# S5 units of a decoder trunk: E turned on TensorE, Toeplitz operand copied out of PSUM, parameter work issued ahead

## The chip, the cores and the metric

One core of a Trainium2 chip runs the whole program. The metric is device time in microseconds: the median of several executions. The profile is that of one further execution.

## The reference

A batch of one, 256 tokens, width 2048, two layers. Layer 0 mixes with an S5 diagonal state space, layer 1 with differential attention on one shared K/V; each layer has a squared-ReLU MLP (2048 to 8192 and back), and sandwich RMS norms stand around every sub-layer. Only the S5 mixer matters here. It has 128 groups of 16 channels with 64 complex states each:

```python
u = (x @ w_in).reshape(Bsz, L, SSM_GROUPS, SSM_GROUP)
# per group: abar = exp(step * lam), bbar = (abar - 1) / lam * b
s_t = abar * s_{t-1} + bbar @ u_t          # complex, 64 states
y_t = Re(c @ s_t) + d_skip * u_t
z = gelu(y)
val, gate = split(z @ w_glu, 2)
mix = val * sigmoid(gate)
```

All matrices are f32, 2048x2048 for w_in and 2048x4096 for w_glu.

## The kernel before

The program is one trace of tile operations. A scheduler at build time orders the instructions of each engine by priority (program order) and by durations that it plans with; at run time every engine's queue is fixed and in order. Work that is ready early can so be placed ahead of work that stands earlier in the program.

In S5, tokens are taken as 32 chunks of 8. Inside a chunk the recurrence is a small matrix (a Toeplitz operand built from a table of the lags 0 to 7); between chunks, states are carried by a scan over 32 chunks.

- Prologue (VectorE): the tables of the groups' parameters: powers of abar (`pw`, written to DRAM as `a_scr` by ScalarE's queue, L447), `Bt`, transposed by TensorE into `T1` and `T2`; chunk rotations `rot`, written to DRAM as `rot_scr`. A zeroed `k_scr` in DRAM is to hold the lag tables; `dskip` holds D on its diagonal.
- `w_in_block(b)`, four of them, each in four steps "W" (L581): u for 512 channels from f32 weights that stream through two buffers (`raw`, on SP's queue, L122), then ScalarE's scaled copy out of PSUM and a VectorE transpose give `Vb`.
- `unit(hh)`, eight of them, 16 groups each, in four steps.
 1. POOL's queue loads `A` (from a_scr) and `B` (from bE); VectorE makes `E` from them (L609 to L612); TensorE multiplies u by E (L615) into `psw`.
 2. POOL loads `cb`; VectorE makes `F` (L627 to L629); TensorE makes the lag table (L634), ScalarE copies it out (`K`, L642), VectorE adds D (L643), and SP's queue writes it to `k_scr` (L645) and reads it back eight times, shifted by a lag each, as the Toeplitz operand `M` (L648).
 3. ScalarE copies psw out (`wsb`, L652), TensorE transposes it into `pst` (L657), and VectorE rotates, scans and rotates back (L667 to L676) and writes the states `ST` (L682, L683). `rt`, the rotations, comes from rot_scr by POOL's queue (L660).
 4. TensorE adds the products with M (L690) and with ST and F (L691) into `psy`, VectorE transposes it (`yT`), ScalarE applies GELU.
- The string `ORDER` gives the program order of W steps and unit steps.
- The GLU follows: `gemm_f32` (L210) takes the first 20 of 32 jobs of its first half in f32 (these need units 0 to 3), all other weights of the trunk are split into a high and a low fp32r part (L137 ScalarE, L138 VectorE) and multiplied at L187 and L188.

The small PSUM tiles of S5 come from one pool of four banks (`mbank`), those of w_in and of the GLU from another of four (`gbank`). The tiles of the units take the memory of the prologue's tiles, and the buffers for split weights take theirs afterwards.

Of the kernel before, what the change touches and what calls it, by code (L numbers as in the profile page):

```python
# [26 lines left out]
ORDER = "WWWW 0000 WWWW 1211122 WW 3 W 2 W 333 WW 4 W 4 W 4455556666 7777"  # L27
P = 128
# [14 lines left out]
def trunk(tc, io, stop=None):  # L43
# [279 lines left out]
    # ------------------------------------------------------------------ S5 layer  # L323
    def s5():
# [14 lines left out]
        dskip = tb.tile([P, 32, SG], F32, name="dskip")  # L339
# [198 lines left out]
        for j in range(4):
            DMA.dma_start(dskip[32 * j : 32 * j + 16], dview(io["d_skip"], j * SG, [[0, 16], [4 * SG, 32], [1, SG]]))
            V.tensor_tensor(  # L540
                dskip[32 * j : 32 * j + 16], dskip[32 * j : 32 * j + 16],
                bc(ident[32 * j : 32 * j + 16, 32 * j : 32 * j + 16], 1, 32), op=MUL,
            )
# [50 lines left out]
        def unit(hh):  # L594
            b, half = divmod(hh, 2)
            par = hh % 2
            g0 = 16 * hh
            Vh = us[b][:, 16 * half : 16 * half + 16, :]
            psw, psk = mbank(), mbank()
            Fs = []  # L600
            for jj in range(2):
# [1 line left out]
                A = ut("A", [8, 2, NS], bufs=2)
                Bq = ut("B", [8, 2, NS], bufs=2)
                a0 = a_scr[0, 0, 0:1]
                nc.gpsimd.dma_start(A.rearrange("p g r n -> p (g r n)"), dview(a0, gj * P, [[G * P, 8], [0, 16], [1, 8 * P]]))
                nc.gpsimd.dma_start(Bq.rearrange("p g r n -> p (g r n)"), dview(io["bE"], gj * P, [[0, 8], [G * P, 16], [1, 8 * P]]))
                E = ut("E", [8, 2, NS])
                V.tensor_tensor(E, bc(A[:, :, 0, :], 2, 2), Bq, op=MUL)  # L609
                V.tensor_tensor(Bq, bc(A[:, :, 1, :], 2, 2), Bq, op=MUL)  # L610
                V.tensor_tensor(E[:, :, 0, :], E[:, :, 0, :], Bq[:, :, 1, :], op=SUB)
                V.tensor_tensor(E[:, :, 1, :], E[:, :, 1, :], Bq[:, :, 0, :], op=ADD)  # L612
# [528 lines left out]
```

## Time and profile before

| | |
|---|---|
| time, median of 3 runs | 2407.84 us (2406.41 to 2408.63) |
| profiled execution, span from first to last instruction | 2406.2 us; its own time is that span and the launch around it, which the record does not give |
| TensorE busy | 2274.4 us (95%) |
| VectorE busy | 1567.2 us (65%) |
| ScalarE busy | 1000.6 us (42%) |
| DMA moved | 432.25 MB, mean 180 GB/s |

Busy shares are means over stages with different limits. The S5 units stand in the first 365 us of the span; everything after them is the GLU's second part, the MLPs, and attention. Read a stage from its own rows: what each engine does there, what it waits for, and what clock TensorE was granted.

### The profile page before, as it was taken

The numbers are of one execution on the slowest core, as the hardware profiler recorded it, in microseconds if no ns is written. First come the engines' busy times: TensorE is split into PE (matmuls) and PEld (weight loads), VectorE is DVE, ScalarE is ACT, GpSimd is POOL, SyncE is SP. The second block draws the span as 40 slices with busy tenths as digits, with TensorE's granted clock in tenths as the row PEclk, the third lists the DMA queues.
The fourth block names the chain that finished last, engine by engine and source line by source line (L and its number), as shares of the span: only waits on it lengthen the run. The fifth ranks groups of instructions, "written<-read, shape, count | busy, mean of one in ns | idle before, by whom it ended". The sixth has DMA issues, their size and how long they took to land.

```text
span 2406.2 us, 32521 instructions
## 1 busy us (share of the span) xinstructions
PE 2274.4 (95%) x13137; PEld 1903.0 (79%) x13137; DVE 1567.2 (65%) x2392; ACT 1000.6 (42%) x1470; POOL 30.4 (1%) x54
## 2 busy tenths in 40 slices
PE   7757689989999999999999999998999999999999
PEld 3335578868888888888868888886888888888887
DVE  8557656867556656656668896656765665665655
ACT  3011125554444444443554455444544444444442
POOL 0100100000000000000000000000000000000000
PEclk9878889999999999999999999999999999999999
DMA  9888976425554554554525544443555555555542
GB/s 282 198 167 159 165 172 248 174 97 210 201 202 173 197 191 174 197 190 158 206 99 188 180 171 162 158 175 123 189 197 210 181 187 192 183 186 192 186 165 104
DMA packets 93943, 432.25 MB, mean 180 GB/s; under 512 B 17377, under 2 KB 39649, under 8 KB 46433
## 3 DMA queue, kind: packets, MB, share of 16 engines
q1 hardware_dynamic: 82624, 405.51, 50.5%
q0 software_dynamic: 9984, 22.04, 4.8%
q10 hardware_dynamic: 1184, 2.62, 0.3%
q8 instruction: 103, 1.69, 0.3%
q14 instruction: 48, 0.39, 0.0%
HBM read 423.44 MB, written 6.68 MB: 179 GB/s over the span
## 4 chain that ended last, share of the span: by engine, by line
PE 85%; DMA 8%; DVE 4%; SPq 1%; ACT 1%; issue 1%; DVEq 0%; ACTq 0%
PE gb L187 47%; PE gb L188 24%; DMA M<-k_scr 4%; DMA raw<-in_w_in_dram 2%; PE gb L184 2%; PE gb L183 2%; PE gb L185 2%; PE mb L256 1%; PE gb L581 1%; DMA k_scr<-K 1%; PE gb L959 1%; PE gb L957 1%; PE gb L958 1%; SPq L648 1%; PE mb L690 1%
## 5 line engine op out<-in xcount | busy, mean ns | idle before, releaser
L138 DVE TENSOR_TENSOR wlo<-raw,whi 128x2048 fp32r<-128x2048 f32 (+1 forms) x540 | 803.1, 1506 | 509.8 <-ACT whi L137 507.6
L137 ACT CAST whi<-raw 128x2048 fp32r<-128x2048 f32 (+1 forms) x540 | 673.3, 1278 | 573.9 <-PE gb L187 375.1
L187 PE MATMUL gb<-x,whi 128*128 128x512 f32 x2400 | 848.8, 398 | 0.0
L188 PE MATMUL gb<-x,wlo 128*128 128x256 f32 x2400 | 675.1, 281 | 0.0
L187 PEld LDWEIGHTS gb<-x,whi 128*128 128x128 f32 x2400 | 450.6, 188 | 109.6
L187 PE MATMUL gb<-xa,whi 128*128 128x512 f32 x1296 | 465.2, 398 | 0.0
L188 PEld LDWEIGHTS gb<-x,wlo 128*128 128x128 f32 x2400 | 453.0, 189 | 0.2
L187 PE MATMUL gb<-xb,whi 128*128 128x512 f32 x1176 | 419.5, 395 | 0.4 <-ACT whi L137 0.4
L188 PE MATMUL gb<-xa,wlo 128*128 128x256 f32 x1296 | 367.8, 284 | 0.0
L188 PE MATMUL gb<-xb,wlo 128*128 128x256 f32 x1176 | 332.0, 283 | 1.6 <-DVE wlo L138 1.6
L187 PEld LDWEIGHTS gb<-xa,whi 128*128 128x128 f32 x1296 | 244.7, 189 | 61.9 <-issue 2.0
L187 PEld LDWEIGHTS gb<-xb,whi 128*128 128x128 f32 x1176 | 221.4, 188 | 52.8 <-issue 2.5
L188 PEld LDWEIGHTS gb<-xa,wlo 128*128 128x128 f32 x1296 | 245.7, 190 | 8.5 <-issue 8.2
L188 PEld LDWEIGHTS gb<-xb,wlo 128*128 128x128 f32 x1176 | 222.9, 190 | 5.2 <-issue 2.9
L215 ACT COPY cr<-gb 128x256 f32<-128x256 f32 x323 | 118.3, 368 | 169.1 <-PE gb L188 167.2
L581 PE MATMUL gb<-raw,h 128*128 128x512 f32 x256 | 122.3, 634 | 23.7 <-DMA raw<-in_w_in_dram 15.6
L162 ACT CAST x<-t 128x256 fp32r<-128x256 f32 x128 | 51.8, 406 | 198.9 <-DVE t L791 174.5
L581 PEld LDWEIGHTS gb<-raw,h 128*128 128x128 f32 x256 | 50.3, 202 | 88.3 <-issue 62.5
L690 PE MATMUL mb<-M,Vb 128*32 128x128 f32 x256 | 36.0, 338 | 76.0 <-DMA M<-k_scr 63.4
L200 DVE TENSOR_TENSOR t<-gb,cr 128x256 f32<-128x256 f32 x151 | 63.1, 418 | 54.9 <-ACT cr L215 54.5
L690 PEld LDWEIGHTS mb<-M,Vb 128*32 128x32 f32 x256 | 19.9, 130 | 82.1 <-issue 78.5
L210 PE MATMUL gb<-z,raw 128*128 128x256 f32 x320 | 72.3, 387 | 2.6 <-DMA raw<-in_w_glu_dram 2.6
(272 smaller groups left out, 2058.5 us busy)
## 6 DMA issues: line engine op xcount, KB each, us to landing
raw<-in_w_up_dram SPq DMA_DIRECT2D x128, 1024.0 KB, 4.7
raw<-in_w_down_dram SPq DMA_DIRECT2D x128, 1024.0 KB, 4.7
raw<-in_w_glu_dram SPq DMA_DIRECT2D x32, 1024.0 KB, 5.1
raw<-in_w_k_dram SPq DMA_DIRECT2D x16, 1024.0 KB, 4.7
raw<-in_w_q_dram SPq DMA_DIRECT2D x16, 1024.0 KB, 4.7
raw<-in_w_v_dram SPq DMA_DIRECT2D x16, 1024.0 KB, 4.7
raw<-in_w_o_dram SPq DMA_DIRECT2D x16, 1024.0 KB, 4.7
raw<-in_w_in_dram SPq DMA_DIRECT2D x15, 1024.0 KB, 10.8
```

What stands on the lines that cost most here:

```text
L137: S.copy(hi[:, c : c + n], raw[:, c : c + n])
L138: V.tensor_tensor(lo[:, c : c + n], raw[:, c : c + n], hi[:, c : c + n].bitcast(F32), op=SUB)
L162: mark[0] = S.copy(dst.hi(dt), src)
L183: T.matmul(ps[:, 0:L], hi[:, c], x.hi(kt), start=f, stop=False)
L184: T.matmul(ps[:, 0:L], hi[:, c], x.lo(kt), start=False, stop=False)
L187: T.matmul(ps, hi[:, c], x.both(kt), start=f, stop=False)
L188: T.matmul(ps[:, L : 2 * L], lo[:, c], x.hi(kt), start=False, stop=l)
L200: V.tensor_tensor(out, ps[:, 0:L], cr, op=ADD)
L210: T.matmul(ps[:, 0:L], w[:, off + kt * P : off + kt * P + P], x[:, kt, :], start=(kt == 0), stop=(kt == nk - 1))
L215: S.copy(cr, ps[:, L : 2 * L])
L581: T.matmul(pss[e], xg[:, kt, e * P : e * P + P], w[:, k4 * 512 : k4 * 512 + 512], start=(kt == 0), stop=(kt == 15))
L690: T.matmul(o, Vh[:, 8 * jj + g, :], M[:, 8 * jj + g, :], start=True, stop=False, tile_position=(0, 32 * g4))
```

## The change

- Parameters: instead of sending the powers of abar through DRAM (`a_scr`, then `A`), TensorE transposes them once, in the prologue, into `AR` and `AI`, which hold them with states on the partitions.
- E: per half unit VectorE forms `X1` (with the states on the partitions) from the b columns of `cb`, which gain a fourth entry (b with its real and imaginary halves swapped), and from AR and AI; TensorE transposes it, eight 128x128 blocks per half unit, and ScalarE copies the result out as `E`. bE is no longer read.
- States: TensorE multiplies E by u directly into `pst` (weights of 64 columns, 32 elements moving), so `psw`, `wsb` and their four transposes go.
- Lag table: 32 columns per matmul instead of 16; the weights are a pair [0, b] or [b, E's lag 1] from `e01`, so that each 32-partition block holds two neighbouring lags. D is added by VectorE in PSUM for both (`dd`). ScalarE then copies the Toeplitz operand `M` straight out of PSUM, 16 copies of 32 partitions, shifted by two lags each; the part of M that is never written was zeroed once by POOL. `k_scr` and `K` go.
- Order: a unit is now `prep` (P, all that needs no u) and `data` (D), and P of a unit stands one or two places ahead of its D. The output matmuls go over four column tiles with M and then four with ST.
- `u` has one buffer instead of two, `Vb` three instead of four.

`rot_scr` and `rt` stay as they are.

```diff
-ORDER = "WWWW 0000 WWWW 1211122 WW 3 W 2 W 333 WW 4 W 4 W 4455556666 7777"
+ORDER = "P0 W W W W P1 W W W W D0 P2 D1 P3 W W W W D2 P4 D3 P5 W W W W D4 P6 D5 P7 D6 D7"
...
         dr = rp("dr", bufs=1, space=DRAM)
-        a_scr = dr.tile([8, G, 2 * NS], F32, name="a_scr")
         rot_scr = dr.tile([P, 2, 64, 32], F32, name="rot_scr")
-        k_scr = dr.tile([G, SG, 15, SG], F32, name="k_scr")
 
...
         rho_n = tb.tile([P, 64], F32, name="rho_n")
-        dskip = tb.tile([P, 32, SG], F32, name="dskip")
...
-        S.dma_start(a_scr.rearrange("d g x -> g d x"), pw[:, 0:8].rearrange("p d r n -> p d (r n)"))
+        nai = ps_.tile([P, 8, NS], F32, name="nai")
+        V.tensor_scalar(nai, pw[:, 0:8, 1, :], -1.0, None, op0=MUL)
+        par = ps_.tile([P, 8, 2, 2, NS], F32, name="par")
+        S.copy(par[:, :, 0, :, :], bc(pw[:, 0:8, 0, :], 2, 2))
+        S.copy(par[:, :, 1, 0, :], nai)
+        S.copy(par[:, :, 1, 1, :], pw[:, 0:8, 1, :])
+        for dst, o in ((AR, 0), (AI, 1)):
+            for d0 in (0, 4):
+                ps = mbank()
+                for i in range(4):
+                    T.transpose(ps[:, i * P : i * P + P], par[:, d0 + i, o].rearrange("p r n -> p (r n)"), ident)
+                S.copy(dst[:, d0 : d0 + 4, :], ps.rearrange("p (d g) -> p d g", g=P))
...
-        zt = ps_.tile([P, SG * 7 * SG], F32, name="zt")
-        V.memset(zt, 0.0)
-        DMA.dma_start(k_scr[:, :, 0:7, :], zt.rearrange("g (p s q) -> g p s q", p=SG, q=SG))
+        pat = ps_.tile([P, 2, SG], F32, name="pat")
+        dskip = ps_.tile([P, 32, SG], F32, name="dskip")
         for j in range(4):
...
+            o = 32 * j
+            S.copy(pat[o : o + 32, 0, :], ident[o : o + 32, o + 16 : o + 32])
+            S.copy(pat[o : o + 32, 1, :], ident[o : o + 32, o : o + 16])
+            DMA.dma_start(dskip[o : o + 32], dview(io["d_skip"], j * SG, [[0, 32], [4 * SG, 32], [1, SG]]))
+        V.tensor_tensor(dd, bc(dskip, 2, 2), bc(pat, 1, 32), op=MUL)
...
+        Mt = [un.tile([P, 16, 8, SG], F32, name=nm("M"), tag=f"M{i}", bufs=1) for i in range(2)]
+        E01 = [un.tile([P, 16, 3, SG], F32, name=nm("E01"), tag=f"E01{i}", bufs=1) for i in range(2)]
+        for i in range(2):
+            GP.memset(Mt[i], 0.0)
+            GP.memset(E01[i][:, :, 0, :], 0.0)
...
-            u = ut("u", [2, 512], bufs=2)
+            u = ut("u", [2, 512], bufs=1)
...
-            Vb = ut("Vb", [32, 32], bufs=4)
+            Vb = ut("Vb", [32, 32], bufs=3)
...
+        def prep(hh):
+            g0 = 16 * hh
             par = hh % 2
-            g0 = 16 * hh
-            Vh = us[b][:, 16 * half : 16 * half + 16, :]
-            psw, psk = mbank(), mbank()
-            Fs = []
+            cb = ut("cb", [16, 4, SG], bufs=2)
+            nc.gpsimd.dma_start(cb, io["cb"][:, g0 * 4 * SG : (g0 + 16) * 4 * SG].rearrange("p (g i q) -> p g i q", i=4, q=SG))
+            e01 = E01[par]
+            psk = mbank()
+            S.copy(e01[:, :, 1, :], cb[:, :, 2, :])
+            Es, Fs = [], []
             for jj in range(2):
                 gj = g0 + 8 * jj
...
-            for jj in range(2):
-                gj = g0 + 8 * jj
-                CR, CI, bS = (cb[:, 8 * jj : 8 * jj + 8, i] for i in range(3))
+                CR, CI, bS, bX = (cb[:, 8 * jj : 8 * jj + 8, i] for i in range(4))
+                X1 = ut("X1", [8, 8, SG], bufs=1)
+                X2 = ut("f2", [8, 8, SG], bufs=2)
+                V.tensor_tensor(X1, bc(bS, 2, 8), bc(AR[:, :, gj : gj + 8].rearrange("p d g -> p g d"), 3, SG), op=MUL)
+                V.tensor_tensor(X2, bc(bX, 2, 8), bc(AI[:, :, gj : gj + 8].rearrange("p d g -> p g d"), 3, SG), op=MUL)
+                V.tensor_tensor(X1, X1, X2, op=ADD)
+                S.copy(e01[:, 8 * jj : 8 * jj + 8, 2, :], X1[:, :, 1, :])
+                E = ut("E", [8, P], bufs=3)
+                for b4 in range(2):
+                    pe = mbank()
+                    for i in range(4):
+                        T.transpose(pe[:, i * P : i * P + P], X1[:, 4 * b4 + i].rearrange("p d q -> p (d q)"), ident)
+                    S.copy(E[:, 4 * b4 : 4 * b4 + 4, :], pe.rearrange("p (g x) -> p g x", x=P))
+                Es.append(E)
                 F = ut("F", [8, 9, SG], bufs=4)
-                f2 = ut("f2", [8, 9, SG], bufs=1)
+                f2 = ut("f2", [8, 9, SG], bufs=2)
                 V.tensor_tensor(F, bc(CR, 2, 9), bc(T1[:, :, gj : gj + 8].rearrange("p d g -> p g d"), 3, SG), op=MUL)
                 V.tensor_tensor(f2, bc(CI, 2, 9), bc(T2[:, :, gj : gj + 8].rearrange("p d g -> p g d"), 3, SG), op=MUL)
                 V.tensor_tensor(F, F, f2, op=ADD)
                 Fs.append(F)
...
+                for sl in (2 * jj, 2 * jj + 1):
+                    for o, n, e0 in ((16, 7, 1), (0, 1, 0)):
+                        for c4 in range(4):
+                            gl = 4 * sl + c4
+                            T.matmul(psk[32 * c4 : 32 * c4 + 32, sl * P + o : sl * P + o + 16 * n],
+                                e01[:, gl, e0 : e0 + 2, :].rearrange("p d q -> p (d q)"),
+                                F[:, gl % 8, 0:n, :].rearrange("p d q -> p (d q)"), start=True, stop=True, tile_position=(0, 32 * c4))
+            kv = psk.rearrange("p (s m q) -> p s m q", s=4, q=SG)
+            V.tensor_tensor(kv[:, :, 0:2, :], kv[:, :, 0:2, :], dd[:, 4 * hh : 4 * hh + 4], op=ADD)
+            M = Mt[par]
+            mv = M.rearrange("p (s c) t q -> p c s t q", c=4)
             for c4 in range(4):
...
+                for j in range(4):
+                    S.copy(mv[32 * j : 32 * j + 32, c4, :, 6 - 2 * j : 8, :], kv[32 * c4 : 32 * c4 + 32, :, 0 : 2 * j + 2, :])
+            held[hh] = Es, Fs, M
+        def data(hh):
+            b, half = divmod(hh, 2)
+            par = hh % 2
+            Es, Fs, M = held.pop(hh)
+            Vh = us[b][:, 16 * half : 16 * half + 16, :]
             pst = mbank()
             for jj in range(2):
-                for ri in range(2):
-                    o = (2 * jj + ri) * P
-                    T.transpose(pst[:, o : o + P], wsb[:, jj, ri].rearrange("p h n -> p (h n)"), ident)
+                for g4 in range(4):
+                    for ri in range(2):
+                        for gh in range(2):
+                            g = 2 * g4 + gh
+                            o = (2 * jj + ri) * P + 32 * g4
+                            T.matmul(pst[64 * gh : 64 * gh + 64, o : o + 32], Es[jj][:, g, 64 * ri : 64 * ri + 64],
+                                Vh[:, 8 * jj + g, :], start=True, stop=True, tile_position=(0, 64 * gh))
             rt = ut("rt", [2, 8, 32], bufs=2)
             r0 = rot_scr[:, :, 8 * hh : 8 * hh + 8, :]
             nc.gpsimd.dma_start(rt, r0)
...
-                for g in range(8):
-                    g4, gh = g // 2, g % 2
-                    o = psy[32 * g4 : 32 * g4 + 32, (2 * jj + gh) * P : (2 * jj + gh) * P + P]
-                    T.matmul(o, Vh[:, 8 * jj + g, :], M[:, 8 * jj + g, :], start=True, stop=False, tile_position=(0, 32 * g4))
-                    T.matmul(o, ST[:, jj, gh, g4, :], Fs[jj][:, g, 1:9, :].rearrange("p d q -> p (d q)"), start=False, stop=True, tile_position=(0, 32 * g4))
+                for gh in range(2):
+                    outs = [psy[32 * i : 32 * i + 32, (2 * jj + gh) * P : (2 * jj + gh) * P + P] for i in range(4)]
+                    for g4 in range(4):
+                        gl = 8 * jj + 2 * g4 + gh
+                        T.matmul(outs[g4], Vh[:, gl, :], M[:, gl].rearrange("p t q -> p (t q)"), start=True, stop=False, tile_position=(0, 32 * g4))
+                    for g4 in range(4):
+                        f = Fs[jj][:, 2 * g4 + gh, 1:9, :].rearrange("p d q -> p (d q)")
+                        T.matmul(outs[g4], ST[:, jj, gh, g4, :], f, start=False, stop=True, tile_position=(0, 32 * g4))
             yT = ut("yT", [2, 8, 32], bufs=1)
             for jj in range(2):
                 V.transpose(yT[:, jj], psy[:, jj * 256 : jj * 256 + 256].rearrange("p (h t q) -> p t h q", h=2, q=SG))
...
-            next(ws if o == "W" else us_[int(o)])
+        for o in ORDER.split():
+            if o == "W":
+                next(ws)
+            elif o[0] == "P":
+                prep(int(o[1]))
+            else:
+                data(int(o[1]))
         uns.close()
         late["small"] = pool("small", bufs=2)
...
-    o["bE"] = np.stack([br, bi], 1).transpose(3, 0, 1, 2).reshape(SG, G * 2 * NS)
-    cb = np.empty((2, NS, G, 3, SG), np.float32)
...
     cb[1, :, :, 2] = bi.transpose(1, 0, 2)
-    o["cb"] = cb.reshape(P, G * 3 * SG)
+    cb[:, :, :, 3] = cb[::-1, :, :, 2]
+    o["cb"] = cb.reshape(P, G * 4 * SG)
     o["d_skip"] = i["ssm_d"][0].reshape(1, D)
     o["w_in"] = lay_a(i["ssm_w_in"][0])
```

## Rows read from the trace of the kernel before

**Rows 1.** The busy time by stage: PE, PEld, DVE, ACT, POOL, clock, DMA share, GB/s.

```profile
50.00:365.00 315.00, 227.12 (x1571) 154.93 (x1569) 189.43 (x272) 52.09 (x101) 26.63 (x43) 0.85 0.87 181
...
480.00:2407.00 1927.00, 1900.02 (x10835) 1633.38 (x10833) 1248.37 (x1836) 870.70 (x1250) 0.00 (x0) 0.99 0.50 175
```

**Rows 2.** The waits of 0:365: us in total, times, longest.

```profile
PE mb L690 <- DMA M<-k_scr: 63.4, 6, 23.0
...
PE gb L581 <- DMA raw<-in_w_in_dram: 15.6, 4, 8.1
...
PE mb L690 <- issue: 11.6, 1, 11.6
```

**Rows 3.** The chain of waits of 0:365, its longest pieces: start, us, what.

```profile
22.63 18.40 DMA raw<-in_w_in_dram
...
151.66 21.88 DMA M<-k_scr
```

**Rows 4.** The waits of SP's queue in 0:420.

```profile
SPq L645 <- DVE K L643: 116.8, 20, 26.9
```

**Rows 5.** The timeline of DVE, its last prologue operation: start, us, what.

```profile
44.99 1.23 DVE L373 TENSOR_TENSOR rot<-ra,rb 128x1024 f32<-128x1024 f32 x1
```

**Rows 6.** The timeline of PE, six places of S5: start, us, what.

```profile
70.90 0.67 PE L615 MATMUL mb<-E,Vb 128*32 128x128 f32 x16
71.49 0.70 PE L581 MATMUL gb<-raw,h 128*128 128x512 f32 x1
...
134.97 0.66 PE L657 MATMUL mb<-ident,wsb 128*128 128x128 f32 x4
135.46 7.03 PE L581 MATMUL gb<-raw,h 128*128 128x512 f32 x16
...
238.73 16.01 PE L210 MATMUL gb<-z,raw 128*128 128x256 f32 x72
...
353.42 0.38 PE L690 MATMUL mb<-M,Vb 128*32 128x128 f32 x2 [1.58 <-DMA M<-k_scr]
...
357.65 6.53 PE L210 MATMUL gb<-z,raw 128*128 128x256 f32 x29
...
365.23 0.73 PE L187 MATMUL gb<-xb,whi 128*128 128x512 f32 x2 [0.41 <-ACT whi L137]
```

**Rows 7.** The groups by line of 0:365: xcount | busy us, mean ns | idle before.

```profile
L581 PE MATMUL gb<-raw,h 128*128 128x512 f32 x256 | 122.3, 634 | 23.7 <-DMA raw<-in_w_in_dram 15.6 <-ACT h L369 6.7 <-issue 1.3
...
L627 DVE TENSOR_TENSOR F<-cb,T 128x1152 f32<-128x1152 f32 x16 | 21.6, 1353 | 70.9 <-PE mb L691 70.9
...
L609 DVE TENSOR_TENSOR E<-A,B 128x1024 f32<-128x1024 f32 x16 | 19.2, 1208 | 4.3 <-DMA B<-in_bE_dram 4.1
L642 ACT COPY K<-mb 16x512 f32<-16x512 f32 x32 | 18.4, 575 | 70.8 <-PE mb L634 70.3
...
L615 PE MATMUL mb<-E,Vb 128*32 128x128 f32 x256 | 11.1, 277 | 0.0
L612 DVE TENSOR_TENSOR E<-E,B 128x512 f32<-128x512 f32 x16 | 10.9, 682 | 0.0
...
L673 DVE TENSOR_TENSOR_SCAN z<-rho,z 128x512 f32<-128x512 f32 x8 | 9.7, 1218 | 0.1
...
L643 DVE TENSOR_TENSOR K<-K,dskip 16x64 f32<-16x64 f32 x32 | 6.8, 214 | 6.2 <-ACT K L642 5.4
...
L682 DVE TENSOR_TENSOR STt<-t,t 64x248 f32<-64x248 f32 x16 | 6.5, 407 | 0.3
...
L196 ACT COPY y<-gb 128x256 f32<-128x256 f32 x10 | 3.7, 371 | 15.1 <-PE gb L210 15.0
```

**Rows 8.** The DMA issues of 0:365: count, KB each, median us to landing.

```profile
raw<-in_w_in_dram SPq DMA_DIRECT2D x15, 1024.0 KB, 10.8
...
A<-a_scr POOLq DMA_DIRECT2D x16, 512.0 KB, 15.0
...
M<-k_scr SPq DMA_DIRECT2D x64, 128.0 KB, 7.4
...
rt<-rot_scr POOLq DMA_DIRECT2D x8, 256.0 KB, 9.1
```

More of the change, by code (lines that the diff above doesn't have):

```diff
@@ L338, in s5 @@
         rho_n = tb.tile([P, 64], F32, name="rho_n")
-        dskip = tb.tile([P, 32, SG], F32, name="dskip")
+        AR = tb.tile([P, 8, G], F32, name="AR")
+        AI = tb.tile([P, 8, G], F32, name="AI")
+        dd = tb.tile([P, 32, 2, SG], F32, name="dd")
         sg = ExitStack()
@@ L533, in s5 @@
         S.dma_start(rot_scr, rot)
-        zt = ps_.tile([P, SG * 7 * SG], F32, name="zt")
-        V.memset(zt, 0.0)
-        DMA.dma_start(k_scr[:, :, 0:7, :], zt.rearrange("g (p s q) -> g p s q", p=SG, q=SG))
+        pat = ps_.tile([P, 2, SG], F32, name="pat")
+        dskip = ps_.tile([P, 32, SG], F32, name="dskip")
         for j in range(4):
[L539 to L543, printed above, removed]
+            o = 32 * j
[3 more added lines that the diff above has]
+        V.tensor_tensor(dd, bc(dskip, 2, 2), bc(pat, 1, 32), op=MUL)
         sg.close()
@@ L592, in w_in_block @@
             yield
-        def unit(hh):
-            b, half = divmod(hh, 2)
+        held = {}
+        def prep(hh):
+            g0 = 16 * hh
             par = hh % 2
-            g0 = 16 * hh
-            Vh = us[b][:, 16 * half : 16 * half + 16, :]
-            psw, psk = mbank(), mbank()
-            Fs = []
+            cb = ut("cb", [16, 4, SG], bufs=2)
[4 more added lines that the diff above has]
+            Es, Fs = [], []
@@ L601, in unit @@
             for jj in range(2):
                 gj = g0 + 8 * jj
[L603 to L612, printed above, removed]
-                for g in range(8):
-                    g4, gh = g // 2, g % 2
-                    T.matmul(psw[32 * g4 : 32 * g4 + 32, (2 * jj + gh) * P : (2 * jj + gh) * P + P],
-                        Vh[:, 8 * jj + g, :], E[:, g].rearrange("p r n -> p (r n)"), start=True, stop=True,
-                        tile_position=(0, 32 * g4),
-                    )
@@ L630, in unit @@
                 Fs.append(F)
-                for g in range(8):
-                    gl = 8 * jj + g
-                    c4, sl = gl % 4, gl // 4
-                    T.matmul(psk[32 * c4 : 32 * c4 + 16, sl * P : sl * P + P],
-                        bS[:, g, :], F[:, g, 0:8, :].rearrange("p d q -> p (d q)"), start=True, stop=True,
-                        tile_position=(0, 32 * c4),
-                    )
-            K = ut("K", [4, 8, SG], bufs=2)
-            for c4 in range(4):
-                q = slice(32 * c4, 32 * c4 + 16)
-                S.copy(K[q], psk[q].rearrange("p (s d q) -> p s d q", s=4, q=SG))
-                V.tensor_tensor(K[q, :, 0, :], K[q, :, 0, :], dskip[q, 4 * hh : 4 * hh + 4, :], op=ADD)
-                k0 = k_scr[0, 0, 0, 0:1]
-                DMA.dma_start(dview(k0, (g0 + c4) * 3840 + 7 * SG, [[240, 16], [4 * 3840, 4], [1, 128]]), K[q].rearrange("p s d q -> p s (d q)"))
@@ L646, in unit @@
-            M = ut("M", [16, 8 * SG], bufs=2)
-            for t_ in range(8):
-                DMA.dma_start(M[16 * t_ : 16 * t_ + 16], dview(k_scr[0, 0, 0, 0:1], g0 * 3840 + t_ * SG, [[240, 16], [3840, 16], [1, 128]]))
-            yield
-            wsb = ut("wsb", [2, 2, 2, NS], bufs=1)
-            S.copy(wsb, psw.rearrange("p (j h r n) -> p j r h n", j=2, h=2, r=2))
+                for sl in (2 * jj, 2 * jj + 1):
[5 more added lines that the diff above has]
+                                F[:, gl % 8, 0:n, :].rearrange("p d q -> p (d q)"), start=True, stop=True, tile_position=(0, 32 * c4))
@@ L683, in unit @@
                 V.tensor_tensor(ST[64:128, :, gh, :, 1:32], t1v[q, :, 1, :, 0:31], t2v[q, :, 0, :, 0:31], op=ADD)
-            yield
             psy = mbank()
             for jj in range(2):
-                for g in range(8):
-                    g4, gh = g // 2, g % 2
-                    o = psy[32 * g4 : 32 * g4 + 32, (2 * jj + gh) * P : (2 * jj + gh) * P + P]
-                    T.matmul(o, Vh[:, 8 * jj + g, :], M[:, 8 * jj + g, :], start=True, stop=False, tile_position=(0, 32 * g4))
-                    T.matmul(o, ST[:, jj, gh, g4, :], Fs[jj][:, g, 1:9, :].rearrange("p d q -> p (d q)"), start=False, stop=True, tile_position=(0, 32 * g4))
+                for gh in range(2):
[6 more added lines that the diff above has]
+                        T.matmul(outs[g4], ST[:, jj, gh, g4, :], f, start=False, stop=True, tile_position=(0, 32 * g4))
             yT = ut("yT", [2, 8, 32], bufs=1)
@@ L755, in s5 @@
         ws = chain(*(w_in_block(b) for b in range(4)))
-        us_ = [unit(hh) for hh in range(8)]
-        for o in ORDER.replace(" ", ""):
-            next(ws if o == "W" else us_[int(o)])
+        for o in ORDER.split():
[5 more added lines that the diff above has]
+                data(int(o[1]))
         uns.close()
@@ L1094, in layouts @@
     br, bi = i["ssm_b_re"][0], i["ssm_b_im"][0]
-    o["bE"] = np.stack([br, bi], 1).transpose(3, 0, 1, 2).reshape(SG, G * 2 * NS)
-    cb = np.empty((2, NS, G, 3, SG), np.float32)
+    cb = np.empty((2, NS, G, 4, SG), np.float32)
     cb[:, :, :, 0] = i["ssm_c_re"][0].transpose(2, 0, 1)
```

4 lines of the change are left out of this document (removed).

## Prediction

> **What bounds the kernel now.** I read the stages first. From 480 us on TensorE is busy 1900 of 1927 us, so nothing that spares other engines can help there; the change touches only the S5 stage, whose end I take to be 365.2 us, the first matmul of the split GLU weights. In 50:365 TensorE is busy 227 of 315 us at a granted clock of 0.85, a mean between its two levels of 1.2 and 2.4 GHz, while the DMA engines are 0.87 busy: this stage is where time can be had, at most the idle 88 us there, something before 50 us, and some half-clock time [rows 1]. The waits then say what TensorE idles for: 63.4 us for M out of k_scr, six times, and an 11.6 us "issue" gap in front of the same matmul, 75 us in all; 15.6 us for w_in chunks [rows 2]. The chain of waits agrees: its longest links are an M load of 21.9 us, one of several, and a w_in load of 18.4 us [rows 3]. SP's own waits show a second harm: it stood 116.8 us in front of the k_scr writes, waiting for VectorE, with the weight loads queued behind [rows 4].
>
> VectorE is second: 189 us in 50:365 [rows 1], after a prologue that ends at 46.2 us with the last rotation [rows 5]. It comes near to bounding the stage once M is gone.
>
> **The change, per unit of 16 groups (8 units).**
>
> TensorE. Packed matmuls on 32 columns of the array, 128 elements moving, go at 37 ns a pass: 16 passes from 70.90 to 71.49 (an f32 matmul is two passes, each a record). Full-width transposes go at 0.122 us: four from 134.97 to 135.46 [rows 6]. The old output matmuls, where M and ST followed each other on one column tile, took 4.2 us for 64 passes (353.42 to 357.65) [rows 6]. After:
> - 16 transposes of E: 16 x 0.122 = 1.96 us. New.
> - lag table: 64 passes instead of 32, half with 112 and half with 16 elements moving: 64 x 0.037 = 2.4 (was 1.2).
> - states directly: 64 passes of 32 elements on 64 columns instead of 32 passes plus 4 transposes. No such shape is in the trace. Below, a quarter of the packed 128-element pass, 0.009: 0.6 us; above, the full-width transpose, 0.122: 7.8 us. I take the packed row's 0.037, 2.4 us: it is the nearest, in column tiles with a contraction of 128, and a pass brings its own weights however little it moves (was 1.2 + 0.5).
> - output: M for four column tiles, then ST for four: packed, 64 x 0.037 = 2.4 (was 4.2).
> Sum 9.1 us against 7.1 at full clock: +2 per unit. TensorE gets more work, not less; the 16 transposes of A in the prologue add 2 us under its wait for w_in.
>
> The trace shows what a visit to a packed shape between full-width ones costs: 16 passes in 0.59 us are 37 ns where a quarter of a 128-element pass at the w_in rate (0.43 us for 512 elements, 16 passes in 7.03 [rows 6]) is 27, so 0.16 us a visit, and that is in my 37 ns. The Trainium skill, TensorEngine Tiling (Array Packing), section Tiling Modes, says that a change of the tiling mode drains the engine, which speaks against a unit that now uses three modes; by it, some four visits more per unit at that 0.16 us would add 5 us to the whole, by my sum none.
>
> VectorE. Gone: the E group, per half of 8 groups two products of 1.21 and two sums of 0.68, so 7.6, and K's four adds, 0.9. New: six 128x1024 products and sums for X1 at 1.21, 7.3, and one add of 128 elements in PSUM, taken at 0.3 (nearest: K's add of 64, 0.21). Kept: F, 6 x 1.35 = 8.1 [rows 7]. So preparation is 15.7 us. The data part stays 8.0: five of 512 elements (four t, Vb) at 0.68, the scan 1.22, eight of about 0.41 (four ST, and two z and two yT of nearly that size). A unit is 23.7 against 24.6 us. The prologue swaps four dskip products of 512 elements (2.7) for dd of 1024 (1.2) and the negation (512, 0.7 at most). VectorE would end its units at 46 + 8 x 23.7 = 236 us if never idle.
>
> ScalarE. Gone: four K copies and wsb, 512 elements each, 5 x 0.58 = 2.9. New: four E evictions of 512 (0.58 each), the e01 copies (0.37 + 2 x 0.27), and 16 shifted copies: per c4 128, 256, 384, 512 elements at 0.27, 0.37, 0.47, 0.58, 6.8 us in all; together 10.0 (0.37 and 0.58 are rows, the others lie on the line through them [rows 7]). So +7.1 a unit, 57 on the 52 us of 50:365, plus some 6 in the prologue: about 110 of 240. Hidden behind VectorE's 23.7; the copies for M are needed only a unit later. If the E evictions queue behind them, it is up to 6.8 us once per unit.
>
> DMA and queues. Gone: 16 loads each of A and B of 512 KB, 64 of M of 128 KB [rows 8], 32 writes of K, the zero fill, a_scr: about 27 MB; cb grows by a third, 1 MB. SP's queue loses 97 issues and their waits, so weight loads leave at once. POOL keeps 8 cb and 8 rt issues and gains four memsets; they may hold the first cb by some microseconds, which VectorE, busy to 46 us, hides; without that cover the first unit starts late by as much. rt still goes through DRAM, as before.
>
> Early: the w_in load that TensorE awaited until 41.0 us was issued at 22.6 and took 18.4 [rows 3]; without A, B and the zero fill beside it I give it the median of the w_in loads, 10.8 [rows 8]: it lands at 33.4. TensorE had begun its 8.1 us wait [rows 2] at 32.9, so block 0, of which 16 passes remain, ends at 33.4 + 16 x 0.43 = 40 us.
>
> **The sum.** TensorE after 40 us: w_in blocks 1 to 3, 192 passes x 0.43 = 82.6; 8 units x 9.1 = 72.5; the f32 half of the GLU, 320 x 0.222 = 71.2 (72 took 16.01 [rows 6]). That ends at 266. Add:
> - waits for weights, 6 (of the 15.6 [rows 2], 7.5 remain beside the early one);
> - half-clock time, 5 (the w_in matmuls alone took 122.3 [rows 7] against 256 x 0.43 = 110);
> - stalls between engines, 14. Each unit's states pass through about 6.4 us of VectorE (four t, two z, the scan, four ST: 2.7 + 0.8 + 1.2 + 1.6) before the output matmuls. Below: nothing, as w_in, the next preparation and the GLU stand ready. Above: 8 x 6.4 = 51. I take a quarter: of the 88 idle us in 50:365, 75 before M and 7.5 before weights leave only 5 for all else, which M's waits may partly have covered.
> So the stage ends at 291 instead of 365.2: 74 us. The split weights themselves were awaited too (0.4 us at 365.23 and some more behind it [rows 6]), at half clock; I put that at 3 us, and it goes as well: weights can be split while the f32 GLU still runs. That is 77 us off the span of 2406.2, which is 2329; the median of the runs lies 1.6 above the span, so **2331 us**.
>
> Does TensorE have cover while VectorE works? The f32 GLU waits for units 0 to 3. VectorE, from 46: five preparations and four data parts, 78.5 + 32 = 110, to 156. TensorE from 40 to then: 82.6 + 5 x 4.4 + 4 x 4.8 = 124, to 164. It just does, with 8 us to spare; from there 71 us of GLU cover the last four units.
>
> **The rivals.**
> 1. The engines alternate: VectorE late by the hand-overs, TensorE idle for all of the 6.4 us in each unit. For: the cover above is only 8 us, and the order is fixed ahead by planned durations, four PSUM banks being shared by all steps. Against: those 5 us. 51 instead of 14: 2368 us. Chance 0.20.
> 2. The wait for M becomes one for rt, which still makes a round trip (9.1 us to landing [rows 8]). Eight of 9 us unhidden instead of the stalls: 2331 + 72 - 14 = 2389. Against: two buffers, and no wait for rt shows now. Chance 0.05.
> 3. Slower: the 64-column state matmuls don't overlap, each pass costing its whole duration, 0.277 us like the record of a packed one [rows 7]. 512 passes x 0.24 = 123 us: 2454. It decides at 0.037 + 77/512 = 0.19 us a pass, above which the gain is gone. Against: packed passes overlap sevenfold now. Chance 0.07 for slower, 0.02 for a price that just cancels.
> 4. The forecast, 0.66, own range 2306 (no stalls, weight waits or half clock; the lower price of the states alone gives 2317) to 2350 (half of rival 1's extra stalls).
>
> By these, faster 0.91, same 0.02 (within 0.2%, about 5 us, what a measurement can tell), slower 0.07. The range for 8 in 10: 2306 to 2374, where the upper end is the transposes' price for the states, 5.4 x 8 = 43 us more, and takes in rival 1.
>
> **What would show it.** Right: no wait for M; the first split GLU matmul near 291 us; 50:290 with TensorE over 85% and a clock above 0.93; DMA share near 0.5; VectorE done with units near 240. Wrong: state matmuls with a start-to-start over 0.1 us; TensorE waiting for t or ST several us in each unit; rt or cb among the waits; the stages behind 480 us changed by more than 2 us.

## The result and the profile after

The changed kernel takes 2310.02 us (median of four runs, 2309.9 to 2312.5) against 2407.84 for the kernel before (median of three runs beside it): a ratio of 0.9599, 95% interval [0.9584, 0.9613]. A fourth run of the kernel before was disturbed (3725 us) and is left out. The profiled execution has a span of 2308.3 us, 97.9 less than before. The forecast of 2331 had the direction and the mechanism, and its range held the time, but the gain came out a quarter larger than the 77 us of its sum.

First the windows of the changed kernel, to be read against [rows 1] (same columns).

```profile
core 0: us, PE busy (x) PEld busy (x) DVE busy (x) ACT busy (x) POOL busy (x), PEclk, DMA share, GB/s
0.00:50.00 50.00, 39.54 (x114) 19.06 (x115) 42.38 (x174) 24.07 (x53) 5.92 (x12) 1.00 0.73 251
50.00:290.00 240.00, 232.65 (x2263) 161.16 (x2262) 195.81 (x242) 116.46 (x253) 9.10 (x14) 0.99 0.45 158
...
405.00:2309.00 1904.00, 1883.71 (x10720) 1618.65 (x10720) 1234.78 (x1810) 859.04 (x1228) 0.00 (x0) 0.99 0.50 176
```

The stage in which TensorE idled for 88 us (50:365) at a granted clock of 0.85 is now busy for 97% of 50:290, at 0.99; the DMA share has halved. The rest of the kernel is what it was: the stage ends (first split GLU matmul) at 267.9 instead of 365.2 us, 97.3 earlier, which is the gain of the span within 0.6 us.

The waits of 0:300 show what replaced those of [rows 2], and SP's own queue what replaced [rows 4] (engine, line, released by, us in total, times, longest).

```profile
PE gb L597 <- DMA raw<-in_w_in_dram: 10.0, 3, 7.0
...
PEld mb L711 <- DVE STt L701: 4.1, 9, 0.8
...
PE mb L711 <- DVE STt L701: 0.5, 2, 0.3
```

```profile
SPq L122 <- PE gb L597: 134.3, 15, 12.1
SPq L122 <- PE gb L210: 91.5, 10, 16.4
```

No wait for M is left, nothing took its place, and 7.0 of the 10 us for w_in are the first load of the program. Up to 267 us SP waits, but for some 7 us in small pieces, only for TensorE to free a weight buffer, which is a queue that runs ahead; nothing in it waits for VectorE's K any more. The forecast priced the stalls before the products with ST at 14 us and its rival at 51: TensorE's weight loads (PEld) wait 4 us for ST, in nine pieces, its matmuls 0.5.

TensorE's timeline of one unit (start, us, instruction, idle before) shows the price of each part. Rows of a packed shape overlap the next, so a price is the distance from one start to the next.

```profile
68.68 0.70 PE L649 MATMUL mb<-F,E 128*32 128x112 f32 x32
69.31 2.84 PE L597 MATMUL gb<-raw,h 128*128 128x512 f32 x6
71.99 1.04 PE L635 MATMUL mb<-ident,X 128*128 128x128 f32 x8
72.86 2.74 PE L597 MATMUL gb<-raw,h 128*128 128x512 f32 x6
...
89.38 2.06 PE L674 MATMUL mb<-Vb,E 128*64 128x32 f32 x64
91.36 0.42 PE L708 MATMUL mb<-M,Vb 128*32 128x128 f32 x8
...
241.92 0.40 PE L711 MATMUL mb<-F,STt 128*32 128x128 f32 x8
242.14 0.40 PE L708 MATMUL mb<-M,Vb 128*32 128x128 f32 x8
...
242.69 23.91 PE L210 MATMUL gb<-z,raw 128*128 128x256 f32 x108
267.89 0.73 PE L187 MATMUL gb<-xb,whi 128*128 128x512 f32 x2 [1.29 <-ACT whi L137]
270.21 0.58 PE L188 MATMUL gb<-xb,wlo 128*128 128x256 f32 x1 [1.59 <-DVE wlo L138]
270.59 0.63 PE L187 MATMUL gb<-xb,whi 128*128 128x512 f32 x1
```

The lag table takes 0.63 us for 32 of its 64 passes (forecast 1.2), the states 1.98 us for 64, 31 ns each (37 forecast, in bounds of 9 and 122), eight transposes 0.87, and eight output passes 0.22 us, so 1.75 for the 64 (forecast 2.4, before 4.2). The group of the state passes, whose records overlap:

```profile
L674 PE MATMUL mb<-Vb,E 128*64 128x32 f32 x512 | 16.5, 223 | 0.0
```

Busy time is the union of overlapping records: 512 state passes of 223 ns each keep TensorE busy for only 16.5 us. Each unit's data part ran with others' work in the gaps, and the units end at 242.8 us with 108 f32 GLU passes (24 us) still to run behind them.

### The profile page after: what moved, and what is told of

It is laid out like the page before. It is cut to its first block, busy times and chain, and to the rows that moved or that the text cites. A ratio compares the mean times of both kernels' runs of the same rounds, so it can differ in the third digit from the quotient of the medians.

```text
span 2308.3 us, 33644 instructions
## 1 busy us (share of the span) xinstructions
PE 2264.3 (98%) x13761; PEld 1895.1 (82%) x13761; DVE 1558.0 (67%) x2349; ACT 1060.4 (46%) x1629; POOL 15.0 (1%) x26
## 4 chain that ended last, share of the span: by engine, by line
PE 87%; DVE 2%; DMA 1%; ACT 0%; issue 0%
PE gb L187 49%; PE gb L188 25%; PE gb L184 2%; PE gb L183 2%; PE gb L185 2%; PE mb L256 1%; PE gb L982 1%; PE gb L981 1%; PE gb L980 1%; PE gb L210 1%; DVE wlo L138 1%; PE mb L941 0%; PE mb L947 0%; DMA raw<-in_w_glu_dram 0%; DVE y L294 0%; DMA raw<-in_w_up_dram 0%
## 5 line engine op out<-in xcount | busy, mean ns | idle before, releaser
L187 PE MATMUL gb<-x,whi 128*128 128x512 f32 x2400 | 848.8, 398 | 0.0
L188 PE MATMUL gb<-x,wlo 128*128 128x256 f32 x2400 | 675.1, 281 | 0.0
L187 PEld LDWEIGHTS gb<-x,whi 128*128 128x128 f32 x2400 | 450.6, 188 | 109.7
L187 PE MATMUL gb<-xa,whi 128*128 128x512 f32 x1296 | 463.7, 397 | 0.0
L188 PEld LDWEIGHTS gb<-x,wlo 128*128 128x128 f32 x2400 | 453.0, 189 | 0.2
L187 PE MATMUL gb<-xb,whi 128*128 128x512 f32 x1176 | 420.7, 396 | 1.3 <-ACT whi L137 1.3
L188 PE MATMUL gb<-xa,wlo 128*128 128x256 f32 x1296 | 367.1, 283 | 0.0
L188 PE MATMUL gb<-xb,wlo 128*128 128x256 f32 x1176 | 332.9, 283 | 1.6 <-DVE wlo L138 1.6
L187 PEld LDWEIGHTS gb<-xa,whi 128*128 128x128 f32 x1296 | 244.0, 188 | 61.3 <-issue 2.0
L187 PEld LDWEIGHTS gb<-xb,whi 128*128 128x128 f32 x1176 | 221.9, 189 | 54.0 <-issue 2.5
L188 PEld LDWEIGHTS gb<-xa,wlo 128*128 128x128 f32 x1296 | 245.1, 189 | 8.5 <-issue 8.2
L188 PEld LDWEIGHTS gb<-xb,wlo 128*128 128x128 f32 x1176 | 223.7, 190 | 5.2 <-issue 2.9
L163 DVE TENSOR_TENSOR x<-t,x 128x256 fp32r<-128x256 f32 x128 | 53.8, 422 | 30.3 <-ACT x L162 30.3
L210 PEld LDWEIGHTS gb<-z,raw 128*128 128x128 f32 x320 | 59.2, 190 | 11.6 <-issue 2.5
```

The costliest lines, as they stand in the source:

```text
L163: mark[1] = V.tensor_tensor(dst.lo(dt), src, dst.hi(dt).bitcast(F32), op=SUB)
L187: T.matmul(ps, hi[:, c], x.both(kt), start=f, stop=False)
L188: T.matmul(ps[:, L : 2 * L], lo[:, c], x.hi(kt), start=False, stop=l)
L210: T.matmul(ps[:, 0:L], w[:, off + kt * P : off + kt * P + P], x[:, kt, :], start=(kt == 0), stop=(kt == nk - 1))
```

## The experiments

Each is an edit of the changed kernel; ratios are to the kernel before, run on the same chip beside it. The changed kernel stands at 0.9599. Differences in us are taken from its 2310.02; by the ratios they come out up to 4 us otherwise (59, 49 and 69 us for runs 1, 3 and 4, where the times say 62, 53 and 73).

**1. The M part undone.** The lag table goes through K and `k_scr` again; preparation still runs ahead, and E is still turned by TensorE.

```diff
-                    S.copy(mv[32 * j : 32 * j + 32, c4, :, 6 - 2 * j : 8, :], kv[...])
+                S.copy(K[q], psk[q].rearrange("p (s d q) -> p s d q", s=4, q=SG))
+                V.tensor_tensor(K[q, :, 0, :], K[q, :, 0, :], dskip[q, 4 * hh : 4 * hh + 4, :], op=ADD)
+                DMA.dma_start(dview(k0, ...), K[q].rearrange("p s d q -> p s (d q)"))
+            for t_ in range(8):
+                DMA.dma_start(M[16 * t_ : 16 * t_ + 16], dview(k_scr[0, 0, 0, 0:1], ...))
```

> The changed kernel with one part undone: the lag table goes through DRAM to M again (16-column lag matmuls, K, k_scr, eight shifted loads), with preparation still issued ahead. Theory 'trip' (TensorE's waits for M were the loss, and the way through DRAM makes them): TensorE waits for M again, at least half of the 98 us comes back, 2355 us or more. Rival 'order' (issuing the parameter work ahead hides the trip by itself): within 10 us of the changed kernel, 2320 or less, no wait for M above 10 us in all. Rival 'load' (A and B, 17 MB, slowed everything): in between, 2320 to 2335, since M brings back only 9 MB.

Measured 2372.43 us, ratio 0.9845 [0.9821, 0.9869]: 62 us of the gain are gone. But TensorE no longer waits for M. Its waits, and then SP's queue:

```profile
PE mb L706 <- DVE STt L696: 48.7, 7, 8.1
PE mb L628 <- DVE X L623: 10.3, 2, 5.5
PE gb L593 <- DMA raw<-in_w_in_dram: 9.5, 1, 9.5
```

```profile
91.27 2.13 SPq L650 DMA_DIRECT2D k_scr<-K  x4
93.50 0.41 SPq L122 DMA_DIRECT2D raw<-in_w_in_dram  x1
96.42 3.97 SPq L653 DMA_DIRECT2D M<-k_scr  x8
115.27 2.05 SPq L650 DMA_DIRECT2D k_scr<-K  x4
```

SP's waits of 0:365 have, in all:

```profile
SPq L650 <- DVE K L648: 107.8, 24, 28.6
```

This is rival 1 of the prediction, at its place and price: 7.0 us per unit for ST (6.4 forecast), 49 us in all (51). The round trip makes it so by way of SP: each unit's K writes wait for VectorE, and from 91 to 187 us only one weight load leaves between the K writes of two units, so the w_in and GLU work that should fill TensorE while VectorE carries the states is not there. The round trip had cost cover, not only M's latency.

**2. The same with K and M on POOL's queue.** This is meant to part the two: the trip stays, the weight loads are no longer behind it.

```diff
-                DMA.dma_start(dview(k0, ...), K[q].rearrange("p s d q -> p s (d q)"))
+                GP.dma_start(dview(k0, ...), K[q].rearrange("p s d q -> p s (d q)"))
-                DMA.dma_start(M[16 * t_ : 16 * t_ + 16], ...)
+                GP.dma_start(M[16 * t_ : 16 * t_ + 16], ...)
```

> The run with M by way of DRAM once more, with the K writes and the M loads issued from POOL's queue instead of SP's; nothing else differs. There TensorE never waited for M, but for ST, and SP issued one w_in load per unit behind each unit's K writes. Theory 'queue' (the trip costs because weight loads stand behind it in SP's queue, so that TensorE has nothing to fill the states' way through VectorE with): 2325 or less, waits for ST under 10 us. Rival 'trip' (the way through DRAM itself, its length or its small packets): 2355 or more.

Measured 2351.4 us, ratio 0.9767 [0.9748, 0.9787], between the two expectations. Waits and windows:

```profile
PE mb L703 <- DMA M<-k_scr: 12.7, 1, 12.7
PE mb L706 <- DVE STt L696: 9.9, 1, 9.9
```

```profile
50.00:290.00 240.00, 211.54 (x1842) 142.30 (x1840) 179.55 (x238) 58.76 (x112) 61.29 (x110) 0.95 0.63 163
290.00:365.00 75.00, 57.96 (x364) 50.33 (x365) 43.70 (x54) 34.68 (x46) 0.00 (x0) 0.84 0.59 194
```

The waits for ST fall from 48.7 to 9.9 us, which points to the order in SP's queue as their cause. Yet only 21 of the 62 us come back. The units now end at 302.9 us instead of 242.8: the f32 GLU is used up beside them, and at the end TensorE waits 12.7 us for an M, with nothing left to run. POOL's own waits of 0:330 show that the run doesn't part the two cleanly:

```profile
POOL k_scr L650 <- DVE K L648: 114.2, 11, 28.5
...
POOL rt L673 <- DVE t L689: 25.0, 6, 4.7
```

The M loads now stand in POOL's queue behind the loads of rt, which wait for VectorE. And the DMA requests change their kind with the queue: the whole run has 68840 packets where run 1 has 84712, and POOL is busy for 61.3 us of 50:290 instead of 9.1. So 21 us is what the move is worth; how the other 41 divide between the way through DRAM and the order in POOL's queue stays open.

**3. The E part undone.** A and B by DMA, psw, wsb and the transposes again; M straight out of PSUM. E and `f2` have a buffer less, to make room.

```diff
+                nc.gpsimd.dma_start(A.rearrange("p g r n -> p (g r n)"), dview(a0, ...))
+                nc.gpsimd.dma_start(Bq.rearrange("p g r n -> p (g r n)"), dview(io["bE"], ...))
+                V.tensor_tensor(E, bc(A[:, :, 0, :], 2, 2), Bq, op=MUL)
...
-                            T.matmul(pst[64 * gh : 64 * gh + 64, o : o + 32], Es[jj][:, g, 64 * ri : 64 * ri + 64], ...)
+                    T.matmul(psw[32 * g4 : 32 * g4 + 32, ...], Vh[:, 8 * jj + g, :], Es[jj][:, g].rearrange("p r n -> p (r n)"), ...)
```

> The changed kernel with the other part undone: E from A and B out of DRAM by VectorE, states by way of psw, wsb and transposes; M stays out of PSUM. E and f2 have one buffer less each, to fit; AR and AI hold only the lags 0 to 3, of which lag 1 is used, with six more small VectorE operations a unit. Theory 'trip': E's loads are not what TensorE waits for; 2335 or less, of which VectorE's extra 8 x 1.8 us and the longer state path are a part. Rival 'load': 2350 or more, w_in loads again near 10 us to landing and TensorE waiting for them.

Measured 2362.79 us, ratio 0.9804 [0.9777, 0.9831]: 53 us lost. My theory, that only M's trip mattered, fell. The waits of TensorE and the window:

```profile
PE gb L599 <- DMA raw<-in_w_in_dram: 30.2, 7, 9.3
PE gb L210 <- DMA raw<-in_w_glu_dram: 12.0, 3, 5.8
PE mb L722 <- DVE STt L712: 8.1, 7, 6.1
```

```profile
50.00:290.00 240.00, 189.65 (x1613) 114.57 (x1612) 174.87 (x259) 73.56 (x167) 25.96 (x42) 0.89 0.70 184
```

The w_in loads (count, KB each, median us from issue to landing):

```profile
raw<-in_w_in_dram SPq DMA_DIRECT2D x15, 1024.0 KB, 9.9
```

Here the harm is mostly load: 42 us of waits for weights, which land after a median of 9.9 us where the changed kernel has 4.8 and the kernel before 10.8 [rows 8]. The longer way of the states and the smaller buffers came with the edit; TensorE's waits show 8.1 us for ST and 1.6 for wsb of them, and no run takes them apart. What slows the loads isn't shown either. It is not the number of small packets alone: in 0:300 run 1 has 26128 under 2 KB and this run 11760, and yet run 1's w_in loads land after 5.7 us.

**4. Both trips kept.** Only the order, the split into prep and data, and the packed output matmuls are new.

> Both ways through DRAM as in the kernel before, only the split into preparation and data, the new order and the packed output matmuls kept. Theory 'trip': 2365 or more, M waits of 40 us or more on TensorE. Rival 'order': 2330 or less. Rival 'load': 2350 or more with the waits on w_in and not on M.

Measured 2382.69 us, ratio 0.9886 [0.9856, 0.9916]. TensorE's waits:

```profile
PE mb L697 <- DVE STt L687: 29.7, 8, 7.3
PE gb L579 <- DMA raw<-in_w_in_dram: 21.6, 7, 8.0
...
PE mb L694 <- DMA M<-k_scr: 6.9, 4, 3.9
```

The time is the one that theory 'trip' expected, the waits are not: those for M are down to 6.9 us, but ST takes 29.7 and w_in 21.6, and the DMA share of 50:290 is 0.99. Undoing M costs 62, E 53, both 73 of the 98 us: the two trips are not two separate costs but two ways of starving the same stage. Of the 25 us that stay, run 6 puts 20 down to the packed output.

**5. Without the lead in program order.**

```diff
-ORDER = "P0 W W W W P1 W W W W D0 P2 D1 P3 W W W W D2 P4 D3 P5 W W W W D4 P6 D5 P7 D6 D7"
+ORDER = "W W W W P0 D0 W W W W P1 D1 P2 D2 W W W W P3 D3 P4 D4 W W W W P5 D5 P6 D6 P7 D7"
```

> The changed kernel with preparation of a unit right before its data part in the program order (W W W W P0 D0 W W W W P1 D1 P2 D2 and so on). Theory 'trip': the scheduler moves ready work ahead by itself; 2310 to 2325. Rival 'order': the lead is what brings the gain; 2345 or more.

Measured 2312.97 us, ratio 0.9595 [0.9573, 0.9618]: no difference that can be told. The lead in the program adds nothing here, which fits a build that places ready work early by itself; splitting the unit so that prep needs no u is not tested apart by this.

**6. The old order of the output matmuls,** M and ST in turn, two groups after each other on one column tile.

```diff
-                    for g4 in range(4):
-                        T.matmul(outs[g4], Vh[:, gl, :], M[...], start=True, stop=False, ...)
-                    for g4 in range(4):
-                        T.matmul(outs[g4], ST[:, jj, gh, g4, :], f, start=False, stop=True, ...)
+                for g in range(8):
+                    T.matmul(o, Vh[...], M[...], start=True, stop=False, ...)
+                    T.matmul(o, ST[:, jj, gh, g4, :], Fs[jj][...], start=False, stop=True, ...)
```

> The changed kernel with the output matmuls in the old order, M and then ST for one group after another. Theory 'TensorE bounds the stage and its packing counts': 64 passes take 4.2 us again instead of 1.75, 2328. Rival 'the order of these matmuls costs nothing, the scheduler orders them anyway': 2312 or less.

Measured 2329.81 us, ratio 0.9678 [0.9659, 0.9697]: 20 us, as 8 x (4.2 - 1.75) says. A fifth of the whole gain is this reordering, which has nothing to do with DRAM.

**7 and 8. More work on one engine.** First each state matmul twice (16 us of TensorE), then one product of F twice (20 us of VectorE).

```diff
+                            for _ in range(2):
                                 T.matmul(pst[64 * gh : 64 * gh + 64, o : o + 32], ...)
```

```diff
+                for _ in range(2):
                     V.tensor_tensor(f2, bc(CI, 2, 9), bc(T2[...]), op=MUL)
```

> The changed kernel with every state matmul issued twice (the second overwrites the first): 64 passes of 31 ns more per unit, 16 us of TensorE in all. Theory 'TensorE bounds the stage now': 2326, plus or minus 3. Rival 'VectorE bounds it': 2313 or less.

> The changed kernel with one product of F computed twice: 16 times 1.27 us start to start, 20 us of VectorE in all. Theory 'TensorE bounds the stage, VectorE has cover': under 2318. Rival 'VectorE bounds it': 2328 or more.

The first took 2330.47 us, ratio 0.9684 [0.9658, 0.9710], 20 us more for 16 (single runs from 2324.9 to 2339.2): TensorE's time counts in full, somewhat above the 2326, plus or minus 3, that I expected. The second took 2326.74, ratio 0.9663 [0.9643, 0.9683], 17 more for 20: there my expectation, that the f32 GLU covers it, fell. TensorE's timeline of the second, its rows with idle time, and the window around them:

```profile
173.21 1.06 PE L635 MATMUL mb<-ident,X 128*128 128x128 f32 x8 [2.33 <-DVE X L629]
178.72 0.66 PE L712 MATMUL mb<-F,STt 128*32 128x128 f32 x8 [4.44 <-DVE STt L702]
184.60 1.39 PE L210 MATMUL gb<-z,raw 128*128 128x256 f32 x4 [2.65 <-ACT z L718]
200.31 8.59 PE L210 MATMUL gb<-z,raw 128*128 128x256 f32 x26 [5.55 <-DMA raw<-in_w_glu_dram]
```

```profile
170.00:210.00 40.00, 25.03 (x319) 20.05 (x321) 32.70 (x43) 20.40 (x49) 2.00 (x3) 0.79 0.24 84
```

Between 170 and 210 us, where w_in is done and the f32 GLU has just begun, TensorE idles 15 us. The two engines are within some microseconds of each other there. The build placed the instructions in another order too, so how much of the 17 us is VectorE's time alone stays open.

**9 to 11. The first split chunk.** The changed kernel's chain of waits (start, us, what) around the end of the stage:

```profile
242.76 16.61 PE gb L210 x76
...
259.39 6.53 DMA raw<-in_w_glu_dram
...
265.94 1.91 ACT whi L137
...
267.87 2.30 DVE wlo L138
```

The first split weights are late because their load waits for a buffer of the f32 jobs. Run 9 gives them their own; runs 10 and 11 also take 14 and 16 f32 jobs in place of 20.

```diff
                 splits.set("gx", gx, 2)
+                raws.n = splits.n = 2
```

```diff
-N32 = 20
+N32 = 14
```

> After the last float32 GLU job the changed kernel's TensorE starts its first split chunk at 267.89 us, waits 1.29 and 1.59 us for that chunk's ScalarE and VectorE pieces, and runs at a lower granted clock until about 275 us; the chain shows that the chunk's load had waited for a raw buffer that the float32 jobs also use. Here the first split chunk has a raw buffer and split buffers of its own, so its load and its split can be done before the float32 jobs end. Theory 'late split': the two waits and the low clock go, about 3 us: 2307. Rival 'nothing there': the wait moves to the second chunk, whose load still waits for the float32 jobs' buffers: 2310 within 1.5 us.

> As the run with the first split chunk's own buffers, and 14 float32 GLU jobs in place of 20. A float32 job is 16 matmuls of 0.222 us = 3.55 us, a split job about 2.8 us; after the units' end at 242.8 us the changed kernel still runs 108 float32 matmuls, 6.75 jobs, which cover nothing but the first split. Theory 'too many float32 jobs': six jobs times 0.75 us less = 4.5 us beside the 3 us of the first split: about 2303. Rival 'they are cover': with 14 the float32 work is used up before the units end, TensorE idles beside them, and the first splits are late: 2310 or more.

> The same with 16 float32 jobs. Theory 'too many float32 jobs': four jobs times 0.75 us = 3 us less beside the 3 us of the first split: about 2304, one or two us above the run with 14. Rival 'they are cover': between 2307 and 2311, and lower than the run with 14.

Run 9 took 2304.08 us, ratio 0.9565 [0.9546, 0.9584], span 2302.3; run 10 2313.65, 0.9607 [0.9588, 0.9626]; run 11 2309.7, 0.9587 [0.9568, 0.9606]. TensorE in run 9, then in run 10:

```profile
243.33 23.58 PE L210 MATMUL gb<-z,raw 128*128 128x256 f32 x108
266.56 0.58 PE L187 MATMUL gb<-xb,whi 128*128 128x512 f32 x1
266.98 0.28 PE L188 MATMUL gb<-xb,wlo 128*128 128x256 f32 x1
267.10 0.39 PE L187 MATMUL gb<-xb,whi 128*128 128x512 f32 x1
```

```profile
241.91 2.86 PE L210 MATMUL gb<-z,raw 128*128 128x256 f32 x12
254.21 1.22 PE L187 MATMUL gb<-xb,whi 128*128 128x512 f32 x2 [9.45 <-ACT whi L137]
256.54 0.58 PE L188 MATMUL gb<-xb,wlo 128*128 128x256 f32 x1 [1.10 <-DVE wlo L138]
```

In run 9 both waits are gone, and so is the slow stretch behind them: an L187 and an L188 matmul together now take 0.34 us from the second pair on (0.54 the first), where the changed kernel needs 0.64 from 270.59 on, to about 275.9. The first L188 matmul with xa, the split z of units 4 to 7, comes at 300.9 instead of 306.7 us. That is 6 us, half of it the two waits and half the slow stretch, twice what I expected, and the best version here; as the runs were made beside different executions of the kernel before, the two intervals just touch, and the rows carry the verdict. Fewer f32 jobs lose it again: with 14, only 12 f32 matmuls are left behind the units, and TensorE waits 9.45 and 1.10 us for the first split. "Too many f32 jobs" fell; they are cover for the first load and split (in that run's chain a load of 7.0 us from 245.22 on, a cast of 1.9, a remainder of 2.3). That load starts 0.4 us after the last f32 matmul, and SP had waited 8.8 us for an f32 job to free a buffer, so a version with fewer f32 jobs whose loads are free of them is not tested.

## Why the prediction was right, and where its sizes were off

- **The mechanism** held: TensorE idled for data that went through DRAM, and SP's queue held the weight loads behind K. Run 1 shows the second, with TensorE idle for ST and not for M, and run 2 that at least 21 of its 62 us are the order in SP's queue, if the move's other effects cost and don't help. That A's and B's load delays weights was said only of the first load; run 3 shows that E's part is worth nearly as much as M's.
- **Block 0** was to end at 40 us and ended at about 44.5 (38 passes of 0.43 from 28.17 on). The wait at 33 us did go, but the sum took over from the kernel before that 48 of the 64 passes are done by then. Now it was 38: TensorE had waited 2.4 us at 18.3 for weights and x and 1.0 us for the tables, and the 16 new transposes (1.8 us) no longer lay under a wait.
- **w_in blocks and f32 GLU**, 82.6 and 71.2, came to 82.3 and 70.8 by the rate of their longest stretches.
- **Units**, 72.5, came to 64.5, by difference: 266.6 (last f32 GLU pass) less 44.5, 82.3, 70.8 and 4.5 idle. The mis-sized terms are the lag table (1.26 a unit, not 2.4) and the output (1.75, not 2.4), and the states and transposes were a little high too; 37 ns held an edge that a longer packed visit pays once. The parts read off the timeline give 6.7 us a unit of the 8.06; I put the other 1.3 down to the edges of the visits, without a run that singles them out. The six w_in passes between two visits take 2.68 us where 6 x 0.43 is 2.58, so about 0.1 us an edge; two of them between two packed visits take 1.06 (91.72 to 92.78), 0.2 above 0.86. The Trainium skill's rule that a change of mode drains the engine (TensorEngine Tiling (Array Packing), section Tiling Modes) agrees in sign with these edges; the 5 us that it added are more than made up by the cheaper passes.
- **Weight waits 6, half clock 5, stalls 14** were the largest error: 25 us, and TensorE idles 4.5 between block 0 and the last f32 GLU pass, and 1.3 before the first split. "A quarter of 51" was a choice between ends; the lower end was right. The weights arrive in time (1.4 us of waits there), the clock is granted in full (1.00) from 44.5 to 266.6 us, and the f32 GLU fills the last four units. The clock fell only after the waits at 267.9.
- **Cover.** The claim that TensorE just suffices while VectorE works, 8 us to spare, was near: f32 GLU began at 163.7 us (forecast from 156 to 164), the units ended at 242.8 (236 at the least). Run 8 shows how thin it is.
- **Split weights, 3 us** to be gained: not obtained, for a reason not looked at, the buffer that they share. Run 9 obtains 6.
- **Rivals.** 1 was not this kernel's, but it is just what appears when the M part is undone. 2 (rt) did not show; of the signs of being wrong, cb stands among the waits, but for 7.3 us of ScalarE's and none of TensorE's. 3 fell clearly: 31 ns against 0.19 us. The stages behind 480 us are unchanged, as said.

Summed: 4.5 later, 8 + 0.7 + 20.5 earlier, 3 not gained gives 22 us less than 2331, against 21 measured. That it closes says little, as the units were taken by difference. And there is luck in the range: with the 29 us alone, without the 4.5 and the 3 that went the other way, the time would have fallen below its lower end of 2306.

## What to carry to other kernels

A round trip through DRAM can cost where the trace shows no wait for it (run 1 has none for M and loses 62 us): its stores wait in a queue with loads that others need, and its traffic can slow those loads (run 3); so put a trip's whole harm (cover, queue, load) into the sum, and expect parts not to add up. When it goes, look for the next late thing at the seam behind the stage: here one buffer count, 6 us. And estimate stalls from whether ready work stands beside them, not as a share of their worst case.

## What was not expected of the hardware

- The order of small f32 matmuls over column tiles alone: 64 passes of 128 elements take 4.2 us with the M and ST matmuls of two groups one after the other on each tile, 1.75 when four tiles take turns, 66 against 27 ns a pass.
- Passes of 32 elements with 64 columns of weights take 31 ns, those of 128 elements on 32 columns 27, and the lag table's, half of 112 and half of 16 elements on 32 columns, 20 on average: the price falls far less than the moving size. How much of the 31 is due to the 64 columns, no run parts.
- A w_in load of 1 MB lands after a median of 4.8 us where the DMA share of 50:290 is 0.45, 6.7 at 0.63 (run 2), 5.7 at 0.67 (run 1), 9.9 at 0.70 (run 3) and 12.8 at 0.99 (run 4): the share alone does not set it.
- After two waits of 1.3 and 1.6 us close together TensorE ran at the lower of its two clock levels for some 6 us (granted clock 0.50 in 270.2:275.9; 0.64 us for a pair of matmuls against 0.34). In run 9, without the waits, it stayed at 1.00 from 266.5 to 277.
